# FFN up projection with a product of 512 columns: both parts of the input under one weight load

## The chip, the cores and the metric

The kernel runs on one NeuronCore of a Trainium2 chip. The metric is the device time of one execution in microseconds (us). Three runs of the kernel before gave 640.26, 641.53 and 641.83 us; the median is 641.53.

The engines go by two names in this text: TensorE (PE in the profile, its weight loads PEld) multiplies matrices and writes to the eight banks of PSUM; VectorE is DVE, ScalarE is ACT, GpSimd is POOL, and SP issues most of the DMAs.

## The reference

A decoder trunk of two layers on 256 tokens with 1024 features. Layer 0 mixes tokens by pooling, layer 1 by a sparse attention with three branches. Each layer is followed by a gated FFN with a causal convolution, and by a gated embedding. Only the FFN is touched by the change:

```python
def conv_ffn(h, w_up, conv_w, conv_b, w_down):      # h: 256 x 1024, normed
    u = h @ w_up                                    # 1024 x 5632
    up = jnp.pad(u, ((0, 0), (CONV_W - 1, 0), (0, 0)))
    u = sum(conv_w[j] * up[:, j:j + S] for j in range(CONV_W)) + conv_b
    a, g = u[..., :D_FF], u[..., D_FF:]             # D_FF = 2816
    return (jax.nn.silu(g) * a) @ w_down
```

Everything is float32, and the result is compared in that precision.

## The kernel before, in words

**Precision.** TensorE multiplies operands of a shorter float type (`F32R`). To keep the precision of float32, each operand is split into a high and a low part, `hi` and `lo = value - hi`, and a product is made of three: high weights times high input, high weights times low input, low weights times high input (`mm3`, line 101). The weights' parts are `wh` and `wl` (made in `ahead`, line 132, from `raw`, which a DMA fills), the input's are `xh` and `xl` (`xsplit`, line 216), the activation's `ah` and `al`, the down weights' `dh` and `dl`. High parts are copies on ScalarE, low parts subtractions on VectorE.

**Layout.** Features lie on the 128 partitions, tokens along the columns. The input of the FFN is 8 tiles (k) of 128 features by 256 tokens. One product of TensorE has 128x128 weights and 256 columns.

**The FFN** (`ffn`, line 322) goes in 22 rounds per layer (`NP`). Round i has a chunk of up weights for 128 features of `a` and 128 of `g` (h = 0 and 1). `begin(i)` takes the chunk and a bank of PSUM, `product(i)` runs 16 steps (2 h by 8 k) of three products into it; the bank holds both halves, 2 x 256 columns, and three banks, 4 to 6, go round. `evac(i)` (line 361) multiplies the bank by the row of the norm (`row`, one factor per token) into `un`, runs the convolution with ScalarE and VectorE, applies silu and splits the result into `ah`, `al`. `down(i)` (line 382) adds the round's 24 products to banks 0 to 3. It runs two rounds later (`LAG`): after `product(i)` come `evac(i)` and `down(i - 2)`.

**The edges.** The norm's row is not needed before the first `evac`: the first product (`KOUT`) goes k by k, as `xsplit` makes the tiles, while `add` collects the squares. `finish` sums them with a product into bank 7, and `rows` spreads the result over the partitions with a product from `dg` (line 253) and copies it to `rrow` (line 283); this is put between the steps of the second product (`FIN`, `NROW`). At the end of a layer's FFN `mixin` injects a first part of the embedding into bank 7 (`inject`, line 441) between `down(20)` and `down(21)`.

**Order.** The text of the program gives each instruction a priority. A scheduler with its own cost model fixes the order within each engine when the program is built; `PR` shifts some priorities (the weight splitting, `'w'`, comes later by 20). On the chip each engine works through its own list in order and waits for semaphores. Buffers and banks go round in the same way: a new owner waits until the readers of the old one are done.

Of the kernel before, what the change touches and what calls it, by code (L numbers as in the profile page):

```python
# [10 lines left out]
F32 = mybir.dt.float32  # L11
F32R = mybir.dt.float32r
# [3 lines left out]
ALU = mybir.AluOpType  # L16
AX = mybir.AxisListType

P = 128
T = 256  # L20
D = 1024
KT = D // P
# [56 lines left out]
def body(ctx, tc, xt, xT, pT, pos, colsd, band, wpool, wup, wdn, wgate, wproj, wkv, wq, wqg, wout,  # L79
         cw1, cw2, out):  # L80
    nc = tc.nc
    V, S, E, G = nc.vector, nc.scalar, nc.tensor, nc.gpsimd
    const = ctx.enter_context(tc.tile_pool(name="const", bufs=1))
    wp = ctx.enter_context(tc.tile_pool(name="wp", bufs=3))
    xp = ctx.enter_context(tc.tile_pool(name="xp", bufs=2))
    sm = ctx.enter_context(tc.tile_pool(name="sm", bufs=2))
    psum = ctx.enter_context(tc.tile_pool(name="psum", bufs=1, space=bass.MemoryType.PSUM))
    fpool = []
# [6 lines left out]
    def bank(i, shape=(P, 2, T), dt=F32):  # L95
        return psum.tile(list(shape), dt, name=f"bank{i}", tag=f"bank{i}")

    def mm(o, w, x, first, last):
        E.matmul(o, w, x, start=first, stop=last, skip_group_check=True)  # L99

    def mm3(o, w, x, first, last):
        for i, (a, b) in enumerate(((0, 0), (0, 1), (1, 0))):
            mm(o, w[a], x[b], first and i == 0, last and i == 2)

    def at(pair, *idx):
        return tuple(t[idx] for t in pair)


    chunks, pooled = [], set()
    for layer in range(2):  # L110
        if layer:
            chunks += [(wkv[k], 1) for k in range(KT)]
            n = len(chunks)
# [33 lines left out]
    def take():  # L147
        ahead(1)
        taken[0] += 1
        w = made[taken[0] - 1]  # L150
        made[taken[0] - 1] = None
        return w
# [15 lines left out]
    x = const.tile([P, KT, T], F32, name="x")  # L168
# [45 lines left out]
        return r  # L214

    def xsplit(src, g, name="x"):
        hi = xp.tile([P, KT, T], F32R, name=name + "h", tag="xh", bufs=2)
        lo = xp.tile([P, KT, T], F32R, name=name + "l", tag="xl", bufs=2)

        def do(k):  # L220
            S.activation(hi[:, k], src(k), AF.Copy, scale=col(g, k))
            V.scalar_tensor_tensor(lo[:, k], src(k), col(g, k), hi[:, k].bitcast(F32),  # L222
                                   op0=ALU.mult, op1=ALU.subtract)
        return (hi, lo), do


    b = bank(7, (P, 512))
# [4 lines left out]
    ub = []  # L232
# [28 lines left out]
        return b[:, 256:]  # L261


    def norm():
        acc = xp.tile([P, T], F32, name="sqa", tag="sqa", bufs=1)

        def add(k):
            if k == 0:
                S.activation(acc, x[:, k], AF.Square)
            else:  # L270
                t = xp.tile([P, T], F32, name="sq", tag="sq", bufs=2)
                S.activation(t, x[:, k], AF.Square)
                G.tensor_tensor(acc, acc, t, op=ALU.add)  # L273

        def finish():
            b = bank(7, (P, 512))
            for i in range(2):
                mm(b[:, i:i + 1], acc[:, i * P:(i + 1) * P], ones[:, 0:1], i == 0, i == 1)
            r = rstd_of(b[:, 0:2], "rcol")

            def rows():
                row = xp.tile([P, T], F32, name="rrow", tag="rrow", bufs=2)
                S.copy(row, row_of(b, r))
                return r, row
            return rows
        return add, finish
# [35 lines left out]
    def ffn(layer, mixin):  # L322
        cn = "conv%d" % layer
        xs, dosplit = xsplit(lambda k: x[:, k], "ffn%d" % layer)
        add, finish = norm()
        ws, up, act = {}, {}, {}
        kout = KOUT[layer]
        n0 = layer * NP
        banks = [4, 5, 6]
        if layer:  # L330
            for i in range(kout):
                ws[i] = take()
                up[i] = bank(banks[i % 3])
        for k in range(KT):
            dosplit(k)
            if layer:
                add(k)
            elif k == 2:
                for i in range(kout):
                    ws[i] = take()  # L340
                    up[i] = bank(banks[i % 3])
        if not layer:
            ahead(1)
            for k in range(KT):
                add(k)
        for k in range(KT):
            if k == KT - 1 and FIN[layer] < 0:
                rows = finish()
            for i in range(kout):
                for h in range(2):  # L350
                    mm3(up[i][:, h], at(ws[i], slice(None), k, slice(h * P, (h + 1) * P)), at(xs, slice(None), k),
                        k == 0 and h == 0, k == KT - 1)
        acc = [bank(i) for i in range(4)]

        def product(i, steps=range(2 * KT)):
            for j in steps:
                h, k = divmod(j, KT)
                mm3(up[i][:, h], at(ws[i], slice(None), k, slice(h * P, (h + 1) * P)),
                    at(xs, slice(None), k), k == 0, k == KT - 1)

        def evac(i):
            un = uns[i % 3]
            V.tensor_tensor(un[:, :, 2:], up[i], row[:, None, :].to_broadcast([P, 2, T]), op=ALU.mult)  # L363
            t = []
            for h in range(2):
                a = COLS[cn][0] + (h * NP + i) * 4
                c = [cols[:, a + j:a + j + 1] for j in range(4)]
                t1 = fpool[0].tile([P, T], F32, name="t1", tag="t1", bufs=4)
                S.activation(t1, un[:, h, 2:], AF.Identity, scale=c[2], bias=c[3])  # L369
                V.scalar_tensor_tensor(t1, un[:, h, 1:T + 1], c[1], t1, op0=ALU.mult, op1=ALU.add)  # L370
                V.scalar_tensor_tensor(t1, un[:, h, 0:T], c[0], t1, op0=ALU.mult, op1=ALU.add)  # L371
                t.append(t1)
            sg = fpool[0].tile([P, T], F32, name="sg", tag="sg")
            S.activation(sg, t[1], AF.Silu)
            V.tensor_mul(sg, sg, t[0])  # L375
            hi = fpool[0].tile([P, T], F32R, name="ah", tag="ah", bufs=LAG + 2)
            lo = fpool[0].tile([P, T], F32R, name="al", tag="al", bufs=LAG + 2)
            S.copy(hi, sg)  # L378
            V.tensor_sub(lo, sg, hi.bitcast(F32))
            act[i] = (hi, lo)  # L380

        def down(i, ds=range(KT)):
            for d in ds:
                mm3(acc[d // 2][:, d % 2], at(dmade[n0 + i], slice(None), slice(d * P, (d + 1) * P)), act[i],
                    i == 0 and d % 2 == 0, i == NP - 1)

        def begin(i):
            ws[i] = take()
            up[i] = bank(banks[i % 3])

        ahead(1)
        begin(kout)
        f, n = max(FIN[layer], 0), NROW[layer]
        product(kout, range(f))
        if FIN[layer] >= 0:
            rows = finish()
        product(kout, range(f, n))
        _, row = rows()
        product(kout, range(n, 2 * KT))
        for i in range(NP):  # L400
            ahead(2)
            if i > kout:
                begin(i)
                product(i)
            evac(i)
            if layer == 0 and i == 6:
                rope_tables()
            if i >= LAG - 1:
                down_weights(n0 + i - LAG + 1)
            if i >= LAG:  # L410
                down(i - LAG)
        down_weights(n0 + NP - 1)
        for i in range(NP - LAG, NP - 1):
            down(i)
        mixin()

        def tail(k):
            if k % 2 == 0:
                down(NP - 1, [k, k + 1])
                V.tensor_add(x[:, k:k + 2], acc[k // 2], x[:, k:k + 2])  # L420
        for k in range(KT):
            tail(k)

    def ple(layer):
# [3 lines left out]
        def mixin():  # L428

            wj[:] = take()  # L430
            ahead(3)
            pj = fp.tile([P, 2, T], F32, name="pj", tag="pj", bufs=1)
            nc.sync.dma_start(pj, pT[:, layer])
            ph[:] = [fp.tile([P, 2, T], F32R, name="ph", tag="ph", bufs=1)]
            pl[:] = [fp.tile([P, 2, T], F32R, name="pl", tag="pl", bufs=1)]
            S.activation(ph[0], pj, AF.Copy, scale=0.5)
            V.scalar_tensor_tensor(pl[0], pj, 0.5, ph[0].bitcast(F32), op0=ALU.mult, op1=ALU.subtract)
            for m in range(PRE):
                inject(m, 7)

        def inject(m, bk, hs=(0, 1)):
            b = bank(bk)
# [73 lines left out]
    def attention_layer(ap):  # L516
# [22 lines left out]
        for k in range(KT):  # L539
            if k == KT - 1:  # L540
                rows = finish()
            w = take()
# [66 lines left out]
        ahead(2)  # L609


        KK = [xp.tile([P, 4, 512], F32R, name="kk", tag=t, bufs=2) for t in ("xh", "xl")]
        KC = ap.tile([P, 2, 4, 16], F32R, name="kc", bufs=1)
        G.memset(KC.bitcast(F32), 0.0)
        half = [slice(0, 64), slice(64, 128)]
# [93 lines left out]

        QQ = [ap.tile([P, 4, 2, T], F32R, name="qq", tag="big", bufs=2) for p in range(2)]  # L710

        OT = [xp.tile([P, 8, T], F32R, name=n, tag=n[:2], bufs=2) for n in ("xho", "xlo")]
        wo = {}

        def product(b, p, m, ks):
# [262 lines left out]

    b = bank(2, (P, 512))
    acc = xp.tile([P, T], F32, name="sqa", tag="sqa", bufs=1)  # L980
    xg = xp.tile([P, KT, T], F32, name="xg", tag="xh", bufs=2)
    sq = xp.tile([P, KT, T], F32, name="sqf", tag="xl", bufs=2)

    def scaled(k):
        S.activation(xg[:, k], x[:, k], AF.Copy, scale=col("final", k))  # L985
# [116 lines left out]
```

## Time and profile before

| | us | share |
|---|---|---|
| the profiled execution | 641.54 | |
| its span, first to last instruction | 639.8 | |
| PE (TensorE products) | 617.2 | 96% |
| PEld (TensorE weight loads) | 583.8 | 91% |
| DVE (VectorE) | 492.5 | 77% |
| ACT (ScalarE) | 369.3 | 58% |
| POOL (GpSimd) | 45.5 | 7% |

The busy time of PE counts overlapping products once. The FFN of layer 0 lies from about 20 to 216 us, that of layer 1 from about 407 to 601 us, the attention between them. The mean granted clock of TensorE over the span is 0.99 of full speed.

### The profile page before, as it was taken

The numbers are of one execution on the slowest core, as the hardware profiler recorded it, in microseconds if no ns is written. First come the engines' busy times: TensorE is split into PE (matmuls) and PEld (weight loads), VectorE is DVE, ScalarE is ACT, GpSimd is POOL, SyncE is SP. The second block draws the span as 40 slices with busy tenths as digits, with TensorE's granted clock in tenths as the row PEclk, the third lists the DMA queues.
The fourth block names the chain that finished last, engine by engine and source line by source line (L and its number), as shares of the span: only waits on it lengthen the run. The fifth ranks groups of instructions, "written<-read, shape, count | busy, mean of one in ns | idle before, by whom it ended". The sixth has DMA issues, their size and how long they took to land. (4 is left out here: it accounts for less than half of the span.)

```text
span 639.8 us, 12056 instructions
## 1 busy us (share of the span) xinstructions
PE 617.2 (96%) x4826; PEld 583.8 (91%) x4826; DVE 492.5 (77%) x852; ACT 369.3 (58%) x688; POOL 45.5 (7%) x69
## 2 busy tenths in 40 slices
PE   8999999999999999999889999999999999999994
PEld 7889999999999999999855666899999999999994
DVE  2999987877777879476998865799777777777844
ACT  3876555555555758363686641785555555555742
POOL 1510000000000313000000000310000000000321
PEclk8999999999999999999989999999999999999998
DMA  8677654445554145756542111367544455553001
GB/s 344 251 279 290 228 187 174 164 181 194 198 198 150 50 149 203 308 180 168 178 112 66 67 67 67 116 231 263 181 177 164 175 194 198 198 185 112 1 2 67
DMA packets 24264, 107.40 MB, mean 168 GB/s; under 512 B 3600, under 2 KB 7696, under 8 KB 15888
## 3 DMA queue, kind: packets, MB, share of 16 engines
q1 hardware_dynamic: 23776, 105.58, 46.3%
q10 hardware_dynamic: 432, 1.05, 0.5%
q8 instruction: 38, 0.62, 0.4%
q14 instruction: 18, 0.15, 0.1%
HBM read 101.80 MB, written 1.05 MB: 161 GB/s over the span
## 5 line engine op out<-in xcount | busy, mean ns | idle before, releaser
L99 PE MATMUL bank<-xl,wh 128*128 128x256 f32 x832 | 236.1, 284 | 0.4 <-DVE xl L222 0.4
L99 PE MATMUL bank<-xh,wl 128*128 128x256 f32 x832 | 235.4, 283 | 0.7 <-DVE wl L144 0.7
L99 PE MATMUL bank<-xh,wh 128*128 128x256 f32 x832 | 235.6, 283 | 0.0
L142 ACT CAST wh<-raw 128x1024 fp32r<-128x1024 f32 (+2 forms) x144 | 141.3, 1002 | 123.2 <-PE bank L99 115.1
L144 DVE TENSOR_TENSOR wl<-raw,wh 128x1024 fp32r<-128x1024 f32 (+2 forms) x142 | 166.2, 1184 | 22.7 <-ACT wh L142 22.6
L99 PEld LDWEIGHTS bank<-xl,wh 128*128 128x128 f32 x832 | 159.1, 191 | 1.7 <-DVE xl L222 0.8
L99 PEld LDWEIGHTS bank<-xh,wl 128*128 128x128 f32 x832 | 159.2, 191 | 1.1 <-DVE wl L144 1.1
L99 PEld LDWEIGHTS bank<-xh,wh 128*128 128x128 f32 x832 | 159.2, 191 | 0.0
L99 PE MATMUL bank<-al,dh 128*128 128x256 f32 x352 | 99.5, 283 | 0.0
L99 PE MATMUL bank<-ah,dl 128*128 128x256 f32 x352 | 99.4, 283 | 0.0
L99 PE MATMUL bank<-ah,dh 128*128 128x256 f32 x352 | 99.4, 282 | 0.0
L363 DVE TENSOR_TENSOR un<-bank,rrow 128x512 f32<-128x512 f32 x44 | 30.4, 690 | 60.2 <-PE bank L99 60.2
L99 PEld LDWEIGHTS bank<-ah,dh 128*128 128x128 f32 x352 | 67.4, 192 | 0.0
L99 PEld LDWEIGHTS bank<-al,dh 128*128 128x128 f32 x352 | 67.4, 191 | 0.0
L99 PEld LDWEIGHTS bank<-ah,dl 128*128 128x128 f32 x352 | 67.4, 191 | 0.0
L273 POOL TENSOR_TENSOR sqa<-sqa,sq 128x256 f32<-128x256 f32 x35 | 29.1, 831 | 401.1 <-issue 375.7
L162 DVE TENSOR_TENSOR dl<-draw,dh 128x1024 fp32r<-128x1024 f32 x44 | 53.6, 1219 | 0.0
L369 ACT ACTIVATE t<-un,cols 128x256 f32<-128x256 f32 x88 | 48.0, 592 | 2.6 <-DVE un L363 2.5
L161 ACT CAST dh<-draw 128x1024 fp32r<-128x1024 f32 x44 | 46.0, 1046 | 3.2 <-DVE x L951 3.2
L378 ACT CAST ah<-sg 128x256 fp32r<-128x256 f32 x44 | 17.9, 406 | 39.1 <-DVE sg L375 39.1
L371 DVE SCALAR_TENSOR_TENSOR t<-un,cols,t 128x256 f32<-128x256 f32 x88 | 38.6, 479 | 0.0
L370 DVE SCALAR_TENSOR_TENSOR t<-un,cols,t 128x256 f32<-128x256 f32 x88 | 38.5, 479 | 0.0
(202 smaller groups left out, 914.1 us busy)
## 6 DMA issues: line engine op xcount, KB each, us to landing
raw<-in_wup SPq DMA_DIRECT2D x44, 1024.0 KB, 4.8
draw<-in_wdn SPq DMA_DIRECT2D x44, 512.0 KB, 4.9
raw<-in_wgate SPq DMA_DIRECT2D x8, 1024.0 KB, 4.8
raw<-in_wkv SPq DMA_DIRECT2D x8, 768.0 KB, 4.2
raw<-in_wq SPq DMA_DIRECT2D x4, 1024.0 KB, 4.8
raw<-in_wout SPq DMA_DIRECT2D x4, 1024.0 KB, 4.9
raw<-in_wproj SPq DMA_DIRECT2D x2, 1024.0 KB, 5.0
w<-in_cw SPq DMA_DIRECT2D x2, 1024.0 KB, 5.8
```

The source lines that it names most:

```text
L99: E.matmul(o, w, x, start=first, stop=last, skip_group_check=True)
L142: S.copy(hi[:, sl], raw[:, sl])
L144: e.tensor_tensor(lo[:, sl], raw[:, sl], hi[:, sl].bitcast(F32), op=ALU.subtract)
L161: S.copy(hi, raw)
L162: V.tensor_sub(lo, raw, hi.bitcast(F32))
L273: G.tensor_tensor(acc, acc, t, op=ALU.add)
L363: V.tensor_tensor(un[:, :, 2:], up[i], row[:, None, :].to_broadcast([P, 2, T]), op=ALU.mult)
L369: S.activation(t1, un[:, h, 2:], AF.Identity, scale=c[2], bias=c[3])
L370: V.scalar_tensor_tensor(t1, un[:, h, 1:T + 1], c[1], t1, op0=ALU.mult, op1=ALU.add)
L371: V.scalar_tensor_tensor(t1, un[:, h, 0:T], c[0], t1, op0=ALU.mult, op1=ALU.add)
L378: S.copy(hi, sg)
```

## The change

The two parts of the input now lie side by side in one tile (`xs`: per k, high and low, 512 columns), and `mm2` replaces `mm3` in the FFN's up projection. The high weights are multiplied with all 512 columns in one product that fills a bank: the first 256 columns are high x high, the second 256 high x low. The low weights are multiplied with the high part and added to the second 256. A round thus has two banks, one for each h, and the two pairs (4, 5) and (6, 7) go round. When a bank is emptied, ScalarE copies its second half to `ub`, VectorE adds the first half to it and then multiplies with the row. The norm's bank becomes 3 in the FFN, that of the first injection 5, and the banks of `down` are taken when they are first written. Other tiles that shared the old tiles' memory (`KK`, `OT`, `xg`) are put into the common one.

```diff
+    def mm2(o, w, x, first, last):
+        mm(o, w[0], x, first, False)
+        mm(o[:, 1], w[1], x[:, 0], False, last)
...
-        hi = xp.tile([P, KT, T], F32R, name=name + "h", tag="xh", bufs=2)
-        lo = xp.tile([P, KT, T], F32R, name=name + "l", tag="xl", bufs=2)
+        both = xp.tile([P, KT, 2, T], F32R, name=name + "s", tag="xs", bufs=2)
+        hi, lo = both[:, :, 0], both[:, :, 1]
...
-            b = bank(7, (P, 512))
+            b = bank(bk, (P, 512))
...
-        add, finish = norm()
+        add, finish = norm(3)
...
-        banks = [4, 5, 6]
+        def begin(i):
+            ws[i] = take()
+            up[i] = [bank(4 + (2 * i + h) % 4) for h in range(2)]
+
+        def step(i, h, k):
+            mm2(up[i][h], at(ws[i], slice(None), k, slice(h * P, (h + 1) * P)), xs[2][:, k], k == 0, k == KT - 1)
...
-        acc = [bank(i) for i in range(4)]
+        acc = {}
...
-                mm3(up[i][:, h], at(ws[i], slice(None), k, slice(h * P, (h + 1) * P)),
-                    at(xs, slice(None), k), k == 0, k == KT - 1)
+                step(i, *divmod(j, KT))
...
-            V.tensor_tensor(un[:, :, 2:], up[i], row[:, None, :].to_broadcast([P, 2, T]), op=ALU.mult)
             t = []
             for h in range(2):
+                ub = fpool[0].tile([P, T], F32, name="ub", tag="ub", bufs=2)
+                S.copy(ub, up[i][h][:, 1])
+                V.tensor_tensor(ub, up[i][h][:, 0], ub, op=ALU.add)
+                V.tensor_tensor(un[:, h, 2:], ub, row, op=ALU.mult)
...
+                if i == 0 and d % 2 == 0:
+                    acc[d // 2] = bank(d // 2)
...
-                inject(m, 7)
+                inject(m, 5)
```

## Rows read from the trace of the kernel before

**Rows 1.** The page's busy times: us, share of the span, instructions.
```profile
PE 617.2 (96%) x4826; PEld 583.8 (91%) x4826; DVE 492.5 (77%) x852; ACT 369.3 (58%) x688; POOL 45.5 (7%) x69
```
**Rows 2.** Waits of PE: who waited for whom, us, times, longest.
```profile
PE bank L99 <- DVE dg L258: 3.8, 3, 1.5
...
PE bank L99 <- DVE wl L144: 0.7, 1, 0.7
...
PE bank L99 <- DVE xl L222: 0.4, 1, 0.4
```
**Rows 3.** Busy time by stretch, layer 0: one round, then 17 rounds.
```profile
core 0: us, PE busy (x) PEld busy (x) DVE busy (x) ACT busy (x) POOL busy (x), PEclk, DMA share, GB/s
120.34:128.95 8.61, 8.61 (x74) 8.61 (x73) 6.44 (x10) 4.76 (x7) 0.00 (x0) 1.00 0.51 176
60.26:206.26 146.00, 146.00 (x1223) 146.00 (x1223) 115.31 (x188) 81.81 (x121) 0.00 (x0) 1.00 0.53 191
```
**Rows 4.** DVE's timeline: start, us, what; in brackets idle before and its releaser.
```profile
120.54 0.69 DVE L363 TENSOR_TENSOR un<-bank,rrow 128x512 f32<-128x512 f32 x1 [1.89 <-PE bank L99]
...
129.15 0.69 DVE L363 TENSOR_TENSOR un<-bank,rrow 128x512 f32<-128x512 f32 x1 [1.89 <-PE bank L99]
```
**Rows 5.** PE's timeline: key/value stage, then scores of the attention.
```profile
268.73 0.40 PE L99 MATMUL bank<-wh,kh 128*128 128x512 f32 x1
...
270.12 0.28 PE L99 MATMUL bank<-kh,wh 128*128 128x256 f32 x1
...
272.99 0.40 PE L99 MATMUL bank<-wh,kh 128*128 128x512 f32 x1
...
342.88 0.73 PE L99 MATMUL bank<-kk,qq 128*128 128x512 f32 x2
343.45 0.28 PE L99 MATMUL bank<-maskb,identb 128*128 128x256 bf16 x1
```
**Rows 6.** Groups of PE by form: out<-in, shapes, count, busy us, mean ns.
```profile
L99 PE MATMUL bank<-xl,wh 128*128 128x256 f32 x832 | 236.1, 284 | 0.4 <-DVE xl L222 0.4
```
**Rows 7.** Timelines of DVE and PE where layer 1's FFN starts.
```profile
408.23 5.37 DVE L222 SCALAR_TENSOR_TENSOR xl<-x,cols,xh 128x256 fp32r<-128x256 f32 x7
...
417.67 0.48 DVE L258 TENSOR_SCALAR dg<-cols,rcol 128x128 f32<-128x128 f32 x2 [0.60 <-POOL rcol L213]
...
418.01 0.71 PE L99 MATMUL bank<-dg,ones 128*128 128x128 f32 x4 [0.93 <-DVE dg L258]
```
**Rows 8.** Groups of ACT and DVE by form, for the prices of emptying.
```profile
L863 ACT COPY ce<-bank 128x256 f32<-128x256 f32 x2 | 0.7, 370 | 2.0 <-PE bank L99 2.0
...
L864 DVE TENSOR_TENSOR ce<-bank,ce 128x256 f32<-128x256 f32 x2 | 0.8, 417 | 0.0
...
L375 DVE TENSOR_TENSOR sg<-sg,t 128x256 f32<-128x256 f32 x44 | 18.4, 419 | 0.0
```
**Rows 9.** ACT's timeline in a round of layer 0.
```profile
129.03 1.05 ACT L142 CAST wh<-raw 128x1024 fp32r<-128x1024 f32 x1 [2.80 <-PE bank L99]
```
**Rows 10.** DVE's `al` and the product that needs it: both FFN starts, one end.
```profile
41.24 0.41 DVE L379 TENSOR_TENSOR al<-sg,ah 128x256 fp32r<-128x256 f32 x1
...
43.00 0.28 PE L99 MATMUL bank<-al,dh 128*128 128x256 f32 x1
...
212.91 0.41 DVE L379 TENSOR_TENSOR al<-sg,ah 128x256 fp32r<-128x256 f32 x1
...
213.68 0.28 PE L99 MATMUL bank<-al,dh 128*128 128x256 f32 x1
...
426.91 0.42 DVE L379 TENSOR_TENSOR al<-sg,ah 128x256 fp32r<-128x256 f32 x1
...
427.90 0.28 PE L99 MATMUL bank<-al,dh 128*128 128x256 f32 x1
```

More of the change, by code (lines that the diff above doesn't have):

```diff
@@ L103, in mm3 @@
             mm(o, w[a], x[b], first and i == 0, last and i == 2)
+    def mm2(o, w, x, first, last):
+        mm(o, w[0], x, first, False)
+        mm(o[:, 1], w[1], x[:, 0], False, last)
     def at(pair, *idx):
-        return tuple(t[idx] for t in pair)
+        return tuple(t[idx] for t in pair[:2])
     chunks, pooled = [], set()
@@ L223, in do @@
                                    op0=ALU.mult, op1=ALU.subtract)
-        return (hi, lo), do
+        return (hi, lo, both), do
     b = bank(7, (P, 512))
@@ L261, in row_of, with norm @@
         return b[:, 256:]
-    def norm():
+    def norm(bk=7):
         acc = xp.tile([P, T], F32, name="sqa", tag="sqa", bufs=1)
@@ L328, in ffn @@
         n0 = layer * NP
-        banks = [4, 5, 6]
+        def begin(i):
[3 more added lines that the diff above has]
+            mm2(up[i][h], at(ws[i], slice(None), k, slice(h * P, (h + 1) * P)), xs[2][:, k], k == 0, k == KT - 1)
         if layer:
             for i in range(kout):
-                ws[i] = take()
-                up[i] = bank(banks[i % 3])
+                begin(i)
         for k in range(KT):
@@ L339, in ffn @@
                 for i in range(kout):
-                    ws[i] = take()
-                    up[i] = bank(banks[i % 3])
+                    begin(i)
         if not layer:
@@ L350, in ffn @@
                 for h in range(2):
-                    mm3(up[i][:, h], at(ws[i], slice(None), k, slice(h * P, (h + 1) * P)), at(xs, slice(None), k),
-                        k == 0 and h == 0, k == KT - 1)
-        acc = [bank(i) for i in range(4)]
+                    step(i, h, k)
+        acc = {}
         def product(i, steps=range(2 * KT)):
             for j in steps:
-                h, k = divmod(j, KT)
-                mm3(up[i][:, h], at(ws[i], slice(None), k, slice(h * P, (h + 1) * P)),
-                    at(xs, slice(None), k), k == 0, k == KT - 1)
+                step(i, *divmod(j, KT))
         def evac(i):
             un = uns[i % 3]
-            V.tensor_tensor(un[:, :, 2:], up[i], row[:, None, :].to_broadcast([P, 2, T]), op=ALU.mult)
             t = []
             for h in range(2):
+                ub = fpool[0].tile([P, T], F32, name="ub", tag="ub", bufs=2)
+                S.copy(ub, up[i][h][:, 1])
+                V.tensor_tensor(ub, up[i][h][:, 0], ub, op=ALU.add)
+                V.tensor_tensor(un[:, h, 2:], ub, row, op=ALU.mult)
                 a = COLS[cn][0] + (h * NP + i) * 4
@@ L383, in down @@
             for d in ds:
+                if i == 0 and d % 2 == 0:
+                    acc[d // 2] = bank(d // 2)
                 mm3(acc[d // 2][:, d % 2], at(dmade[n0 + i], slice(None), slice(d * P, (d + 1) * P)), act[i],
                     i == 0 and d % 2 == 0, i == NP - 1)
-        def begin(i):
-            ws[i] = take()
-            up[i] = bank(banks[i % 3])
         ahead(1)
@@ L609, in attention_layer @@
         ahead(2)
-        KK = [xp.tile([P, 4, 512], F32R, name="kk", tag=t, bufs=2) for t in ("xh", "xl")]
+        KK = xp.tile([P, 2, 4, 512], F32R, name="kk", tag="xs", bufs=2)
+        KK = [KK[:, i] for i in range(2)]
         KC = ap.tile([P, 2, 4, 16], F32R, name="kc", bufs=1)
@@ L710, in attention_layer @@
         QQ = [ap.tile([P, 4, 2, T], F32R, name="qq", tag="big", bufs=2) for p in range(2)]
-        OT = [xp.tile([P, 8, T], F32R, name=n, tag=n[:2], bufs=2) for n in ("xho", "xlo")]
+        OT = xp.tile([P, 2, 8, T], F32R, name="xo", tag="xs", bufs=2)
+        OT = [OT[:, i] for i in range(2)]
         wo = {}
@@ L980, in body @@
     acc = xp.tile([P, T], F32, name="sqa", tag="sqa", bufs=1)
-    xg = xp.tile([P, KT, T], F32, name="xg", tag="xh", bufs=2)
-    sq = xp.tile([P, KT, T], F32, name="sqf", tag="xl", bufs=2)
+    xg = xp.tile([P, 2, KT, T], F32, name="xg", tag="xs", bufs=2)
+    xg, sq = xg[:, 0], xg[:, 1]
     def scaled(k):
```

## The prediction

> **What bounds the kernel now.** I read the busy times first: TensorE is busy 617.2 of 639.8 us, VectorE 492.5, ScalarE 369.3 [rows 1]. Next what TensorE waits for: its largest groups are 3.8 us for `dg` (the row of the norm), 0.7 for `wl`, 0.4 for `xl` [rows 2], so hardly anything but its own length is left. Then the stretches: from 60 to 206 us, inside the FFN of layer 0, it is busy all the time at a granted clock of 1.00, that is at the 2.4 GHz level, with VectorE at 115.3 of 146.0 us and ScalarE at 81.8 [rows 3]. The FFN thus costs what its products cost in a row. Their price is the distance of starts, not the 283 ns that one lasts (they overlap): one round of `evac` to the next is 8.61 us [rows 4] and holds 48 up and 24 down products, so 8.61/72 = 119.6 ns each. The profiled execution took 641.54 us, 1.7 around its span of 639.8; the median is 641.53, so I count from 641.5.
>
> **What is removed on TensorE.** Per step (one k, one half h) three products of 256 columns become one of 512 and one of 256. The key/value stage has both widths side by side: six products of 512 columns take from 268.73 us to the first narrow one at 270.12, 231.7 ns apiece, and the 24 of 256 from there to the next wide one at 272.99, 119.6 ns apiece [rows 5]. A step falls from 3 x 119.6 = 358.7 to 231.7 + 119.6 = 351.3 ns, 7.5 ns less. Columns stay what they were; what goes is the fixed share of one product and its weight load. Both stretches hold a change of width, so a change adds no gap of its own. The ends of this price: at 2.4 GHz 256 columns are 106.7 ns, and if all of the 12.9 ns beyond were per instruction, a step would save 12.9. At the other end two score products of 512 columns, after other shapes, take (343.45 - 342.88)/2 = 285 ns each [rows 5], 46 ns more per step and some 30 us in all. I take the key/value rows: the same element type, the same dense stream, while the score products come between waits; their end stays outside the range, counted with the slower cases.
>
> There are 44 x 16 = 704 steps (the 832 products of each kind include 128 of the gates [rows 6]). Not all shorten the run. The first product of each layer is fed k by k as `xl` is made, seven in 5.37 us or 767 ns each [rows 7], against 717 ns for the six old products of one k: it goes at VectorE's pace before and after. The steps between it and the wait for `dg` (10 in layer 0, 3 in layer 1) only lengthen that wait, 1.5 and 0.93 us now [rows 2, 7]. That leaves 704 - 32 - 13 = 659 steps, and 659 x 7.5 ns = **4.9 us**.
>
> The Trainium skill, "TensorE: Matmul & The Clock Gate", section "Back-to-back issue gap", gives N/2.4 + 2.5 ns per product on the warm clock, which leaves 2.5 ns for a removed one; by it the sum would be an estimated 659 x 2.5 = 1.6 us. The trace disagrees: from 256 to 512 columns it shows 112.1 ns more and 7.5 beside them, where that formula has 106.7 and 2.5.
>
> **What is added on VectorE and ScalarE.** Per round one multiply of 512 columns out of the bank (0.69 us [rows 4]) becomes two copies on ScalarE, two additions and two multiplies of 256. Nearest rows: copy out of a bank 0.37, addition with one operand in a bank 0.42, a product within SBUF 0.42 [rows 8]. VectorE: 6.44 busy per round [rows 3] - 0.69 + 4 x 0.42 = 7.43 of a new round of 8.61 - 16 x 0.0075 = 8.49 us. ScalarE: 4.76 + 2 x 0.37 = 5.5. Both stay under TensorE's round, so in the steady stretch they cost nothing; the cover is VectorE's wait of 1.89 us per round for the bank [rows 4]. Behind the new copies stand the weight casts on ScalarE, which today wait 2.80 us per round for TensorE [rows 9]. Each half now has its own bank, so the first half's copy, addition and multiply can go into these two waits, before the product ends.
>
> **What moves in PSUM.** The ring shrinks from three products deep to two. Product i needs the pair that round i-2 emptied: between the end of product i-2 and its start lie one round and one down product, 8.49 + 2.87 = 11.4 us, while emptying takes about 2 (two copies, two additions, one after the other 1.6). No cost until VectorE is some 9 us late. The norm's bank (7 to 3), the injection (7 to 5), the late `acc` and the common tile for both parts of x have nothing queued behind them that is late today; I cost them at nothing. Without the cover each would wait for its bank to be emptied, those 2 us once.
>
> **The edges, where VectorE has no slack.** At both FFN starts it works without a gap, and down(0) needs `al` of round 0. Layer 1: `al` ends at 427.33, its product starts at 427.90 [rows 10], 0.57 spare. Two rounds of emptying lie before it, each 0.99 longer; the additions of round 0 can run before the row exists (VectorE idles 0.60 there [rows 7]), so I take 1.1 us of delay (ends: 0 and 2.0), and TensorE arrives 29 x 0.0075 = 0.2 earlier: 0.7 us lost. Layer 0: `al` ends at 41.65, wanted at 43.00 [rows 10], 1.35 spare: nothing lost (at most 0.8). An addition caught in front of `dg` can delay the row by up to 0.42 per layer, I take 0.2 each. At the ends `al` of round 21 is done at 213.32 for a product at 213.68 [rows 10]; the second half's chain is 0.37 + 0.42 + 0.42 - 0.69 = 0.52 longer, against 0.36 spare, less what the early first half frees: 0.1 per layer. Together **1.3 us** (ends 0 and 3.5).
>
> Sum: 641.5 - 4.9 + 1.3 = **637.9 us**. With the ends of the edges 636.6 to 640.1; with 12.9 ns per step (8.5 us) and no edge cost 633.0.
>
> **Rivals.**
> A. More than I count is per instruction: 12.9 ns, 8.5 - 1.3 gives 634.3. For it: columns at 2.4 GHz; against it: the wide rows.
> B. No change. What a removed product frees is small, 2.5 ns per step, 1.6 - 1.3 gives 641.2; the page's formula above works out this way. Or the edges take 3.5 and a newly ordered attention layer (the order written by the scheduler follows its own clock) another 1, 641.1. For it: a saving of only 2% of a step; against it: the rows of 231.7 ns.
> C. Slower: VectorE becomes the bound. The new chain copy, addition, multiply crosses engines twice inside strict queues. If each half's addition waits for a copy that stands behind one cast of 1.05 us [rows 9], the round needs 7.43 + 2 x 1.05 = 9.53 us, and TensorE waits in all but the first rounds: 40 x (9.53 - 8.61) = +37, some 678 us. It decides from 1.06 us of new waiting per round; one such wait does not reach it. For it: VectorE's 88% of a round; against it: the waits above that the chain can use.
> That the change doesn't do what it says would show as 2112 up products again; the diff leaves no room for it.
>
> **Chances.** Forecast 0.60 (636.6 to 639.5), A 0.10, B 0.18, C 0.12. What a measurement of this kernel tells from no change is 0.3%, 1.9 us: faster means under 639.6. Forecast and A nearly all count as faster, 0.70; same 0.19; slower 0.11. The range runs from A without edge costs to B's middle, 633.0 to 641.0, and leaves out C and the upper part of B.
>
> **What will show it.** Right: 704 products of 512 columns starting 351 ns a pair with the narrow one, a round of 8.49 us, TensorE's waits in the FFN stretches still zero, VectorE about 7.4 per round. Wrong: a pair at 359 ns or more (price), a round above 8.61 with TensorE waiting for a bank, `al` or `wl` (C), or a gap at down(0) of several us (edges).

## The result, and the profile after

The changed kernel takes 632.78 us (median of 4 runs, 632.36 to 634.92) against 640.89 for the kernel before (4 runs): a ratio of 0.9877, 95% interval 0.9858 to 0.9897. That is 8.1 us less, where 3.6 were forecast, and 0.2 us below the range. The profiled execution fell from 641.54 to 632.52 us, its span from 639.8 to 630.7.

First the page's busy times, which answer to [rows 1]:

```profile
PE 609.0 (97%) x4122; PEld 544.7 (86%) x4122; DVE 536.2 (85%) x984; ACT 403.7 (64%) x776; POOL 45.1 (7%) x69
```

704 products are gone (4826 to 4122), VectorE has 44 us more, and TensorE still bounds the kernel at 97%. What it waits for, beside [rows 2]:

```profile
PE bank L99 <- DVE dg L264: 3.0, 3, 1.4
```

The wait for `dg` is 0.8 us smaller than before, not larger. Two of the three waits are at the FFN's starts, 1.18 and 0.43 us after 1.50 and 0.93 before; the third, 1.35 in both kernels, is at the kernel's end. Next the stretches, beside [rows 3]: 16 rounds of layer 0 and 17 of layer 1, and two shorter stretches for the clock.

```profile
core 0: us, PE busy (x) PEld busy (x) DVE busy (x) ACT busy (x) POOL busy (x), PEclk, DMA share, GB/s
8.00:20.00 12.00, 11.46 (x69) 10.56 (x70) 8.96 (x18) 6.83 (x15) 4.38 (x7) 1.00 1.02 414
60.53:195.47 134.94, 134.94 (x899) 124.31 (x897) 127.79 (x230) 91.25 (x148) 0.00 (x0) 1.00 0.57 206
320.00:360.00 40.00, 35.86 (x212) 22.45 (x211) 35.14 (x93) 26.86 (x104) 0.00 (x0) 1.00 0.26 79
438.28:581.65 143.37, 143.37 (x955) 132.07 (x953) 131.70 (x228) 96.48 (x154) 0.00 (x0) 1.00 0.54 194
```

TensorE is busy all the time, as forecast. A round takes 134.94/16 = 143.37/17 = 8.43 us; VectorE is busy for 7.75 (layer 1) to 7.99 of it (forecast 7.43), ScalarE for 5.7. TensorE's timeline of one round shows the price itself: the first product of the round, the next two, the round's first `down` product, and the next round.

```profile
119.57 0.39 PE L99 MATMUL bank<-xs,wh 128*128 128x512 f32 x1
...
119.92 0.40 PE L99 MATMUL bank<-xs,wh 128*128 128x512 f32 x1
120.15 0.28 PE L99 MATMUL bank<-xs,wl 128*128 128x256 f32 x1
...
125.12 0.28 PE L99 MATMUL bank<-ah,dh 128*128 128x256 f32 x1
...
128.00 0.39 PE L99 MATMUL bank<-xs,wh 128*128 128x512 f32 x1
```

From 119.57 to 125.12 lie 16 steps, 347 ns each; the 24 `down` products take the other 2.88 us, as before. The round of before is 8.607 us (17 distances in its trace; the 146.00 us of [rows 3] are 0.3 short of 17 such rounds), so a step has become (8.607 - 8.433)/16 = 10.9 ns cheaper, not 7.5. The emptying costs what its nearest rows said [rows 8], by the groups of the three new instructions:

```profile
L374 ACT COPY ub<-bank 128x256 f32<-128x256 f32 x88 | 32.0, 367 | 40.9 <-PE bank L99 40.8
...
L375 DVE TENSOR_TENSOR ub<-bank,ub 128x256 f32<-128x256 f32 x88 | 36.5, 419 | 0.5
L376 DVE TENSOR_TENSOR un<-ub,rrow 128x256 f32<-128x256 f32 x88 | 36.6, 419 | 0.1
```

To place the time I cut each profiled execution at the starts of TensorE's own marks: the last `us,wpl` product of the token mixing, the first key/value product (the end of layer 0 with its FFN), the last product of the attention's output (`xo`, `xho` before), the last `ah,dh` product, the end.

| us | start | FFN, layer 0 | attention | FFN, layer 1 | end | span |
|---|---|---|---|---|---|---|
| before | 20.7 | 223.9 | 162.3 | 194.1 | 38.8 | 639.8 |
| changed | 19.1 | 220.5 | 162.0 | 190.4 | 38.8 | 630.7 |

The two FFN stages give 3.4 + 3.7 = 7.1 us. The 1.6 at the start are not the change's. Here is the kernel before in the same two short stretches:

```profile
8.00:20.00 12.00, 11.55 (x60) 10.85 (x61) 7.29 (x15) 6.16 (x14) 3.33 (x4) 0.86 1.03 422
320.00:360.00 40.00, 35.71 (x190) 21.00 (x189) 34.95 (x88) 27.48 (x104) 0.00 (x0) 0.96 0.29 79
```

From 8 to 20 us, busy for 11.55 of the 12, it had a granted clock of 0.86, so it spent a part of the stretch at the lower level of 1.2 GHz; in the changed kernel it was 1.00, 2.4 GHz throughout. Such falls come and go between executions of one kernel: where the mean clock was at its highest, 0.992, the kernel before took 640.05 to 640.36 us in 11 runs, the changed one 632.36 to 633.05 in 5, medians 640.26 and 632.71. At an equal clock the change is thus worth 7.5 us.

### The profile page after: what moved, and what is told of

It reads as the page before. It is cut to its first block, busy times and chain, and to the rows that moved or that the text cites. A ratio compares the mean times of both kernels' runs of the same rounds, so it can differ in the third digit from the quotient of the medians.

```text
span 630.7 us, 10850 instructions
## 1 busy us (share of the span) xinstructions
PE 609.0 (97%) x4122; PEld 544.7 (86%) x4122; DVE 536.2 (85%) x984; ACT 403.7 (64%) x776; POOL 45.1 (7%) x69
## 5 line engine op out<-in xcount | busy, mean ns | idle before, releaser
L99 PE MATMUL bank<-xs,wh 128*128 128x512 f32 (+1 forms) x960 | 295.4, 365 | 0.4 <-DVE xs L228 0.2
L99 PE MATMUL bank<-xs,wl 128*128 128x256 f32 x832 | 233.6, 281 | 0.6 <-DVE wl L149 0.6
L99 PEld LDWEIGHTS bank<-xs,wh 128*128 128x128 f32 x960 | 171.8, 189 | 30.2 <-DVE xs L228 3.1
L99 PEld LDWEIGHTS bank<-xs,wl 128*128 128x128 f32 x832 | 157.5, 189 | 1.3 <-DVE wl L149 1.3
L380 ACT ACTIVATE t<-un,cols 128x256 f32<-128x256 f32 x88 | 52.4, 601 | 10.0 <-DVE un L376 9.8
L166 ACT CAST dh<-draw 128x1024 fp32r<-128x1024 f32 x44 | 46.2, 1052 | 19.1 <-PE bank L99 16.0
L374 ACT COPY ub<-bank 128x256 f32<-128x256 f32 x88 | 32.0, 367 | 40.9 <-PE bank L99 40.8
L167 DVE TENSOR_TENSOR dl<-draw,dh 128x1024 fp32r<-128x1024 f32 x44 | 53.6, 1218 | 0.0
L381 DVE SCALAR_TENSOR_TENSOR t<-un,cols,t 128x256 f32<-128x256 f32 x88 | 42.0, 481 | 5.4 <-ACT t L380 5.1
L382 DVE SCALAR_TENSOR_TENSOR t<-un,cols,t 128x256 f32<-128x256 f32 x88 | 42.0, 482 | 1.6
L375 DVE TENSOR_TENSOR ub<-bank,ub 128x256 f32<-128x256 f32 x88 | 36.5, 419 | 0.5
L376 DVE TENSOR_TENSOR un<-ub,rrow 128x256 f32<-128x256 f32 x88 | 36.6, 419 | 0.1
L99 PE MATMUL bank<-qs,wh 128*128 128x256 f32 x144 | 28.6, 294 | 0.0
```

Of the source, the lines that this page charges most:

```text
L166: S.copy(hi, raw)
L167: V.tensor_sub(lo, raw, hi.bitcast(F32))
L374: S.copy(ub, up[i][h][:, 1])
L375: V.tensor_tensor(ub, up[i][h][:, 0], ub, op=ALU.add)
L376: V.tensor_tensor(un[:, h, 2:], ub, row, op=ALU.mult)
```

## The experiments

**1. Does the saving need the alternation of widths?** Per half, eight wide products, then eight narrow ones, in place of pairs:

```diff
-                step(i, *divmod(j, KT))
+                h, r = divmod(j, 2 * KT)
+                k, w = r % KT, ws[i][r // KT][:, r % KT, h * P:(h + 1) * P]
+                if r < KT:
+                    mm(up[i][h], w, xs[2][:, k], k == 0, False)
+                else:
+                    mm(up[i][h][:, 1], w, xs[2][:, k, 0], False, k == KT - 1)
```

> The same 704 wide and 704 narrow products of the up projection, but in each half eight wide ones in a row, then eight narrow ones in a row (the first product of a layer stays in pairs). Theory T1: a narrow product directly behind another narrow one is held to about 119.6 ns by the load of its weights, behind a wide one it is free of that and takes 116.7; only the alternation gives the extra saving. Then narrow behind narrow goes back to 119.6, a wide one stays at 230 to 232, a step costs 350 to 351 ns as I had reckoned from the key/value rows, and with some 640 grouped steps the time is 2.3 to 3 us above the changed kernel, about 635.5 us. Rival T2: the order plays no part, the key/value stage's wide products were dear for a reason of their own; then a step stays at 346.7 ns and the time at 632.8 us.

Measured: 636.95 us (635.28 to 639.27, 6 runs), ratio 0.9935 [0.9913, 0.9957]. The time alone would have confirmed that grouping is dearer. TensorE's timeline in a round says otherwise (a row with x8 starts eight products; the next row's start ends them):

```profile
122.71 1.99 PE L99 MATMUL bank<-xs,wh 128*128 128x512 f32 x8
124.53 1.11 PE L99 MATMUL bank<-xs,wl 128*128 128x256 f32 x8
125.49 2.00 PE L99 MATMUL bank<-xs,wh 128*128 128x512 f32 x8
127.33 1.11 PE L99 MATMUL bank<-xs,wl 128*128 128x256 f32 x8
```

Wide products are 227.5 and 230 ns apart, narrow ones 120: 348 per step, a round of 8.44 us, and the FFN of layer 1 took 190.6 us against 190.4. The order of widths plays next to no part. The time went elsewhere. The FFN stage of layer 0 is 1.7 us longer (222.2), nearly all of it ahead of the steady rounds: TensorE's wait for `dg` there was 2.3 us instead of 1.2, and its clock from 20 to 45 us was 0.93; whether the longer wait is the edit's own is not shown. The rest is the clock in stretches that the edit does not touch, 0.86 from 8 to 20 us and, in the attention:

```profile
320.00:360.00 40.00, 36.47 (x182) 22.33 (x182) 33.32 (x85) 26.14 (x97) 0.00 (x0) 0.89 0.25 70
```

Its start was 20.7 us long, like that of the kernel before, and its attention 164.1, 2.1 more than the changed kernel's.

**2. Is it the wide product, or the new banks and the new emptying?** The wide product split in two again, all else as changed:

```diff
-        mm(o, w[0], x, first, False)
+        mm(o[:, 0], w[0], x[:, 0], first, False)
+        mm(o[:, 1], w[0], x[:, 1], False, False)
```

> The changed kernel with the wide product undone alone: high weights times high part and high weights times low part are two products of 256 columns again, into the two halves of the same bank; banks, emptying, tiles and all else stay as changed. If the whole gain comes from the wide product, a step is back at 358.7 ns and the time is that of the kernel before plus what the emptying costs at the edges: 641 to 642.5 us. Rival: the separate banks for each half or the earlier emptying give part of the gain; then it stays under 639.5 us.

Measured: 642.07 us (640.43 to 643.17, 12 runs), ratio 1.0014 [1.0002, 1.0026] to the kernel before. The group and the starts of two rounds:

```profile
L99 PE MATMUL bank<-xs,wh 128*128 128x256 f32 x1664 | 303.9, 284 | 0.2 <-DVE xs L229 0.2
```

```profile
454.79 0.28 PE L99 MATMUL bank<-xs,wh 128*128 128x256 f32 x1
...
463.39 0.28 PE L99 MATMUL bank<-xs,wh 128*128 128x256 f32 x1
```

The round is 8.60 us again, the FFN stages 224.1 and 194.5 us. So the whole gain is the wide product, and the new emptying and banks cost 0.1 to 1.7 us by the interval.

**3. What does a product cost by its width?** At the end of layer 0, 216 extra products in rows of one width, or of two in turn; their results are not used.

> The changed kernel with 216 extra products at the end of layer 0's FFN, whose results are not used: 24 each in a row of 256, 512, alternating 512 and 256, 384, 128, alternating 512 and 128, 64, alternating 512 and 64, and 256, 512, 512 by turns. Read from the distances of their starts. T1 (weight loads set a pace of their own): a row of 128 or 64 columns does not get cheaper than the load's pace, far above its columns' share (53 or 27 ns), while behind a wide one the same product is cheap; from these the pace of the load can be read. T2 (a fixed cost per product, no separate pace): 128 columns about 65 ns, 64 about 38, and the same behind a wide one.

One run, 669.17 us with the extra products. TensorE's timeline; each block is two merged rows of 12, named by the first product in it, and the next row's start ends it:

```profile
208.25 1.60 PE L99 MATMUL bank<-xs,wl 128*128 128x256 f32 x12
209.69 2.91 PE L99 MATMUL bank<-xs,wh 128*128 128x512 f32 x12
212.44 2.88 PE L99 MATMUL bank<-xs,wl 128*128 128x512 f32 x12
215.16 2.27 PE L99 MATMUL bank<-xs,wh 128*128 128x512 f32 x12
...
219.39 2.28 PE L99 MATMUL bank<-xs,wh 128*128 128x384 f32 x12
221.51 2.24 PE L99 MATMUL bank<-xs,wl 128*128 128x384 f32 x12
223.59 1.45 PE L99 MATMUL bank<-xs,wh 128*128 128x128 f32 x12
224.87 1.50 PE L99 MATMUL bank<-xs,wl 128*128 128x128 f32 x12
226.21 2.22 PE L99 MATMUL bank<-xs,wh 128*128 128x512 f32 x12
...
230.31 1.47 PE L99 MATMUL bank<-xs,wh 128*128 128x64 f32 x12
231.62 1.50 PE L99 MATMUL bank<-xs,wl 128*128 128x64 f32 x12
232.96 2.21 PE L99 MATMUL bank<-xs,wh 128*128 128x512 f32 x12
```

The first products of a block still carry the change of width: the first twelve wide ones take (212.44 - 209.69)/12 = 229.2 ns each, the second twelve 226.7. So I read the second twelve: 120.0 ns at 256 columns, 173.3 at 384, 226.7 at 512, and 111.7 at 128 as at 64. At 2.4 GHz the columns are 106.7, 160.0 and 213.3 ns, so from 256 columns on the same 13.3 ns lie beyond them: this share goes with the product and not with its columns. Whether it is the product's own or that of its weight load is not shown, as every product here has a load. 512 and 256 in turn, both into the start of the bank, take 352.5 per pair (215.16 to 219.39), 512 and 128 take 341.7 (226.21 to 230.31). A narrow product behind a wide one is thus not cheap, as T1 had it, and neither 65 nor 38 ns, as T2 had it. And the wide product is 226.7 here, not 231.7.

**4. Why are the wide products of the key/value stage dearer [rows 5]?** Seven blocks of extra products, results unused: (1) wide in a row into one bank; (2) the bank changed every three, as in that stage; (3) the operands' roles as in that stage (weights from the input tile); (4) both; (5) pairs as in the FFN, the narrow product into the second half of the bank; (6) the same into the first half; (7) as 5, with another k.

> The changed kernel with extra products at the end of layer 0's FFN whose results are not used, in blocks parted by two products of 64 columns: (1) 24 wide ones, weights and input as in the up projection, one bank; (2) the same, bank changed after every three; (3) 24 wide ones with the roles of the key/value stage (weights from the input's tile, columns from the weights' tile), one bank; (4) the same, order and bank changed after every three as in that stage; (5) 12 pairs as in the FFN, wide, then narrow into the second half; (6) pairs with the narrow one into the first half; (7) pairs where the narrow one takes another k of the input. Known: the grouped kernel has 228 to 230 ns for a wide one, the key/value stage 231.7 in every run. If the roles of the operands make it dear: blocks 1, 2 at 228, blocks 3, 4 at 231.7. If the change of bank does: blocks 2 and 4 at 231.7, 1 and 3 at 228. If neither: all at 228. Pairs: 347 ns in block 5; if the output half or another k accounts for the 352 ns that alternating products took in the block of widths, blocks 6 or 7 show 352.

One run, 671.93 us. The second halves of blocks 1 and 2 and the 64-column products between the blocks (x14 are two of these and 12 of block 2), then the last 21 products of block 3 and of block 4, in views that start behind the first ones:

```profile
211.02 2.88 PE L99 MATMUL bank<-xs,wl 128*128 128x512 f32 x12
213.74 3.12 PE L99 MATMUL bank<-xs,wh 128*128 128x64 f32 x14
216.69 2.88 PE L99 MATMUL bank<-xs,wl 128*128 128x512 f32 x12
219.41 0.30 PE L99 MATMUL bank<-xs,wh 128*128 128x64 f32 x2
...
220.33 4.92 PE L99 MATMUL bank<-wh,xs 128*128 128x512 f32 x21
225.09 0.30 PE L99 MATMUL bank<-xs,wh 128*128 128x64 f32 x2
...
226.00 4.92 PE L99 MATMUL bank<-wh,xs 128*128 128x512 f32 x21
230.76 0.62 PE L99 MATMUL bank<-xs,wh 128*128 128x64 f32 x3
```

Block 1: (213.74 - 211.02)/12 = 226.7 ns. Block 2: (219.41 - 216.69)/12 = 226.7. Blocks 3 and 4: (225.09 - 220.33)/21 and (230.76 - 226.00)/21, 226.7 each. So neither a change of bank nor the other roles make a wide product dearer, the third of the expected cases. A mean over the whole of a block would mislead: in blocks 2 to 4 the first wide product, behind two of 64 columns, has the next one 0.32 us after it, and this alone lifts the mean to 230.4 to 230.8. What makes the key/value stage's six dear is what stands ahead of them. They follow narrow products; here are the starts between the first, 268.73, and the narrow one at 270.12 [rows 5], in the kernel before:

```profile
268.96 0.40 PE L99 MATMUL bank<-wh,kl 128*128 128x512 f32 x1
269.20 0.39 PE L99 MATMUL bank<-wl,kh 128*128 128x512 f32 x1
269.43 0.40 PE L99 MATMUL bank<-wh,kh 128*128 128x512 f32 x1
269.66 0.39 PE L99 MATMUL bank<-wh,kl 128*128 128x512 f32 x1
269.89 0.39 PE L99 MATMUL bank<-wl,kh 128*128 128x512 f32 x1
```

To the nanosecond the trace has 233, 236, 229, 232, 231 and 227 between them. The wide row of experiment 3, in one bank and with the FFN's roles, opens behind narrow products in nearly the same way: 233, 236, 228, 233, 231, 226, and then stays at 226.7. A run-in of nearly 30 ns in all is thus in the mean of the six; why it is there is open. The FFN's pairs measured 347 ns (ten pairs from 231.33 to 234.80), the sum of the steady 226.7 and 120.0, and 353 with the narrow product into the first half, which accounts for the 352.5 of experiment 3; another k, 347. Why the first half is dearer is open.

**5. How much more can VectorE take?** The multiplication by the row done twice, 0.84 us more per round:

```diff
                 V.tensor_tensor(un[:, h, 2:], ub, row, op=ALU.mult)
+                V.tensor_tensor(un[:, h, 2:], ub, row, op=ALU.mult)
```

> The changed kernel with the multiplication by the row done twice in each half (the second result is written over the first, so the FFN's input of the convolution is the same): 2 x 0.42 us more on VectorE per round. In the changed kernel VectorE is busy 131.7 of 143.4 us in layer 1's steady stretch, 7.75 us of a round of 8.43. If VectorE has only what lies between these two, 0.68, it becomes the bound: 8.59 us a round, some 0.16 x 40 = 6 us more, 639 us. If its queue hides less than that because its waits lie at the wrong places, more: up to 0.84 x 40 = 34 us. Rival: the weight splitting runs so far ahead that the excess never reaches TensorE: 633 to 634 us.

Measured: 637.83 us (637.42 to 639.0, 4 runs), ratio 0.9951 [0.9931, 0.997]. 17 rounds of layer 1:

```profile
444.65:587.90 143.25, 143.25 (x953) 131.96 (x952) 137.79 (x260) 91.74 (x155) 0.00 (x0) 1.00 0.54 194
```

VectorE is at 8.11 of 8.43 us and the round has not moved. Its busy time rose by 0.36 us per round and not by 0.84: where its instructions stand in a row, each starts some 0.08 us before the one ahead has ended, and busy time counts the overlap once. The bound of 8.59 that I expected had left this out. The FFN stages are 1.3 (221.8) and 1.7 us (192.1) longer than in the changed kernel, all of it outside the steady rounds, and another 2.1 us are in the attention (164.1), at a clock of 0.91 from 320 to 360 us. So even a longer emptying is hidden in the steady rounds, and what it costs is paid at the edges.

**6. A later place for the norm's row.** `NROW = (13, 4)` for `(10, 3)`, so that more steps of the second product come ahead of the wait for `dg`.

> The changed kernel with NROW = (13, 4) for (10, 3): three more steps of the second product in layer 0, one more in layer 1, stand ahead of the wait for the norm's row (dg), where TensorE idles 1.18 and 0.43 us in the changed kernel. Theory: this idle time is lost time, 3 x 0.347 + 0.347 = 1.4 us less, 631.4 us. Rival: the first emptying hangs on the row and VectorE is full there, so TensorE then waits for al of round 0 at down(0) instead: 632.8 us, no change.

Measured: 634.57 us (633.09 to 635.59, 6 runs), ratio 0.9885 [0.9861, 0.991], as the changed kernel's own beside it (experiment 8). It decides nothing: TensorE's and VectorE's instructions stand in the same order as in the changed kernel, so the edit moved nothing. The run is a second measurement of the changed kernel. Its profile had a clock of 0.86 from 8 to 20 us and a start of 20.8 us, like the kernel before, with the FFN stages at 220.4: the 1.6 us at the start come and go without any edit.

**7. A faster version? The multiplication by the row on GpSimd**, except in the last round:

```diff
-                V.tensor_tensor(un[:, h, 2:], ub, row, op=ALU.mult)
+                (V if i == NP - 1 else G).tensor_tensor(un[:, h, 2:], ub, row, op=ALU.mult)
```

> The changed kernel with the multiplication by the row on GpSimd, except in the last round: 0.84 us less on VectorE per round, two products of 256 on GpSimd at some 0.83 us each (what its sums of squares take). One such multiplication more on VectorE cost 1.3 to 1.5 us per FFN, all at its edges. Theory (VectorE's load at the FFN starts sets the edge cost): taking one pair away gives up to that back, 0.5 to 1.3 us per FFN, 630 to 632 us. Rival: GpSimd's longer product lengthens the chain to al, or its reads slow VectorE's own: 633 to 635 us.

Measured: 655.05 us (653.11 to 657.53, 6 runs), ratio 1.0209 [1.018, 1.0239]: slower. TensorE's first wait, then groups of GpSimd and VectorE:

```profile
PE bank L99 <- ACT ah L389: 12.6, 7, 2.9
```

```profile
L376 POOL TENSOR_TENSOR un<-ub,rrow 128x256 f32<-128x256 f32 x84 | 107.3, 1281 | 242.6 <-DVE ub L375 239.4 <-ACT rrow L289 3.1
...
L167 DVE TENSOR_TENSOR dl<-draw,dh 128x1024 fp32r<-128x1024 f32 x44 | 69.9, 1588 | 0.0
...
L386 DVE TENSOR_TENSOR sg<-sg,t 128x256 f32<-128x256 f32 x44 | 33.3, 757 | 7.4 <-ACT sg L385 7.4
```

A multiply that VectorE does in 419 ns takes GpSimd 1281, and VectorE's own work slows beside it: `dl` from 1218 to 1588 ns, `sg` from 422 to 757. The 757 is a mean of two kinds. With GpSimd idle a `sg` product takes 407 to 426 ns; in most rounds it starts some 0.13 us after a multiplication of GpSimd and takes 883 to 899 (at 121.09 us, behind one that runs from 120.96 to 121.71). It ends some 0.28 us after GpSimd does, which looks like a wait and not like a slower rate; two others took 415 and 419 with GpSimd at work, so the rule is not shown. `ah` comes late and TensorE waits.

**8. The changed kernel again**, beside experiments 4, 6 and 7.

> The changed kernel once more, unaltered, beside the others on the same chip, so that small differences have a base: 632.4 to 633 us where TensorE's clock does not fall in the first 20 us, some 1.6 us more where it does, as in the profiled execution of the kernel before.

Measured: 634.84 us (6 runs; 632.71 and 632.90 at a mean clock of 0.992, the rest 634.76 to 635.35 at 0.987 to 0.990) against 641.74 before, ratio 0.988 [0.9852, 0.9908]. Its profiled execution was one of the latter, with a lower clock in the attention:

```profile
320.00:360.00 40.00, 36.26 (x192) 22.78 (x193) 33.17 (x87) 25.58 (x93) 0.00 (x0) 0.91 0.26 79
```

Its FFN stages (220.5 and 190.3) repeat the first profile's; the attention differs, 164.2 against 162.0, and the end by 0.5. The 2.1 us that experiments 1 and 5 show in the attention are therefore not their edits'. I had expected falls of the clock at the start alone.

## Why the prediction was wrong, step by step

- **TensorE bounds the kernel, and a step is worth its products in a row**: right. It is busy without a gap in the steady stretch before and after, and without the wide product the gain is gone (experiment 2).
- **The price of a step: the step that failed.** Forecast 351.3 ns, 7.5 saved; measured 347, 10.9 saved. I took the wide product from the key/value rows, 231.7 ns. Those six are the first behind narrow products, and a run-in of nearly 30 ns is in their mean; in a steady row it is 226.7, in whichever bank and roles, and with the steady narrow one, 120.0, the pair is 346.7 (experiments 3 and 4). The sentence that a change of width adds no gap of its own was the misreading: I had looked at the mean of the six and not at their starts one by one. Over 659 steps the difference is 659 x 3.4 = 2.2 us. The upper end, 12.9 ns, was near the truth, and rival A (634.3), which I gave 0.10, came out: counted on the profiled execution, 641.5 less the 7.1 of the FFN stages is 634.4. The argument against A, "the wide rows", was the error: they showed the width together with a run-in that the FFN's pairs do not have.
- **The count of steps**: 659 x 10.9 = 7.2 us against 7.1 in the two stages. It holds, if the edges cost next to nothing; the two are measured only together.
- **The edges, the second term that was off**: forecast 1.3 us, measured 7.2 - 7.1 = 0.1 net. Layer 1's `al` is not late. In layer 0 it would have been:

```profile
41.83 0.64 PE L99 MATMUL bank<-ah,dh 128*128 128x256 f32 x4
42.30 0.39 PE L99 MATMUL bank<-xs,wh 128*128 128x512 f32 x1
...
43.00 0.28 PE L99 MATMUL bank<-al,dh 128*128 128x256 f32 x1
```

  `al` ends at 42.67 (VectorE, from 42.25 for 0.42), 0.37 us after the four `ah` products that began at 41.83 have gone, but the new order has four up products in between, and nothing waits. The wait for `dg` became 0.8 us shorter, where I had added 0.4. At the layers' ends the later `ah` costs more than the 0.1 I took: the last product before down(21) starts at 208.30, the next at 208.72, a gap of 0.42 against some 0.12 in a row, and the same in layer 1. I priced the old order with new durations; the scheduler wrote a new one.
- **The emptying is hidden; two pairs of banks are enough**: right, with VectorE at 7.75 to 7.99 instead of 7.43 per round, and room for 0.84 more (experiment 5). Rival C is refuted by the same run: waits chained across engines did not lengthen the round. Rival B is refuted by the round.
- **The Trainium skill, "TensorE: Matmul & The Clock Gate", section "Back-to-back issue gap"**, gives N/2.4 + 2.5 ns, by its own words for an isolated product; for a stream in which each product has its weight load it gives about 81 ns at 128 columns and 131 at 512. The trace disagrees with both: a removed product brought 10.9 ns, and the rows of experiment 3 show 111.7 ns at 128 columns and 226.7 at 512, 13.3 beyond the columns.
- **The base**: 641.5 us held a fall of the clock of 1.6 us at the start. The forecast's 3.6 plus 2.2 (price), 1.2 (edges), 1.6 (clock) and 0.3 (attention) is 8.9 of the 9.0 between the two profiled executions. With the price and the edges as measured, the forecast from the same base would have been 634.4, inside the range; that the time came out 0.2 us below the range is the base's doing. At equal clock 0.4 us (7.5 against 7.1) are left; 0.3 of it lies in the attention, of which one execution of each kernel does not tell whether it is the change's.

## What to carry to other kernels

Take a price from starts one by one, and from where their distances have become steady, not from the mean of the first few behind another width: a run-in of 5 ns per product, times hundreds of instructions, was the larger part of what the forecast missed in the FFN. Before a time of some 0.5% is given to an edit, compare the granted clock and the length of the stages that the edit does not touch: experiment 1's time agreed with a theory that its own trace refutes. The same holds for an experiment with extra products: the ones put in as marks changed the mean of the blocks behind them. Edges are set by an order that the scheduler writes anew, so a sum made with the old order there is a bound, not a forecast.

## What the runs showed of the hardware that was not expected

- In this stream, with a weight load for each product, a product in a steady row costs 111.7 ns at 64 columns as at 128, 120.0 at 256, 173.3 at 384 and 226.7 at 512: from 256 columns on, 13.3 ns more than its columns at 2.4 GHz (experiment 3).
- The first wide products behind narrow ones are dearer: 233, 236, 229, 232, 231 and 227 ns in the key/value stage. Neither a new bank every three products nor weights and input swapped changes the steady 226.7 (experiment 4). A narrow product behind a wide one costs 6 ns more when it goes into the first half of the bank instead of the second (353 against 347 per pair). The causes are open.
- A VectorE product within SBUF that starts while GpSimd multiplies there takes 883 to 899 ns in most rounds, and 407 to 426 with GpSimd idle (experiment 7).
